# A hybrid decoder step on one core: the layer norms' rows written by ScalarE, row sums four at once, history products later

## The chip, the cores and the metric

The kernel runs on one core of a Trainium2 chip. The core has a matrix engine (TensorE: PE in the profile, with PEld for its weight loads), VectorE (DVE), ScalarE (ACT), GpSimd (POOL) and the queue engine SyncE (SP), which issues DMAs here. Each engine takes its own instructions in order, and semaphores hold one engine back for another. The metric is the device time of one execution in microseconds (us), as the median of several runs.

## The reference

The step computes two layers for 512 new prompt positions and 8 sampled sequences with one new token each, with a model width of 1024. Layer 0 mixes tokens by sliding-window attention, layer 1 by gated linear attention (GLA). Behind each mixer, and behind each gated convolutional feed-forward block (ConvFFN), stands a residual addition with a layer norm. There are four such norms, and they are what is changed:

```python
def layer_norm(x, g, b):
    mu = jnp.mean(xf, -1, keepdims=True)
    var = jnp.mean(jnp.square(xf - mu), -1, keepdims=True)
    return (xf - mu) * lax.rsqrt(var + LN_EPS) * g + b

def conv_ffn(x, buf, w_up, conv_w, conv_b, w_down):
    h = x @ w_up
    a, u = h[..., :D_FF], h[..., D_FF:]            # D_FF = 2816
    ap = jnp.concatenate([buf, a], axis=1)         # buf: the last 2 rows, the history
    c = conv_b + sum(conv_w[j] * ap[:, j:j + T] for j in range(3))
    return (gelu(c) * u) @ w_down, ap[:, T:]

for i in range(2):
    m = swa(x) if i == 0 else gla_mix(x)
    x = layer_norm(ALPHA * x + m, ln_mix_g[i], ln_mix_b[i])
    f, new_buf = conv_ffn(x, ...)
    x = layer_norm(ALPHA * x + f, ln_ffn_g[i], ln_ffn_b[i])
```

## The kernel before

**Layout.** The activations lie transposed: features on the 128 partitions, in 8 chunks of 128 features, and positions along the free dimension. Positions come in two groups: group a has 256 prompt positions, group b has 256 and the 8 sampled tokens (264 columns). For each group `g.x` holds the rows in f32; a high and a low part of each (`xh` and `xl`, for group a both in `xs`, in the type fp32r) feed TensorE. A weight is split in the same way (`wh`, `wl`), and a product is three matmuls for each chunk: high by high, high by low, low by high. The columns of the parts are stored in two halves by parity; `parted` and `even` are that view.

**Order.** The work is a list of units, one for each 128 columns of a weight; `order` runs each unit for group a some units ahead of group b (the lead). Generators (`spawn`, `yield n`) run a unit's later work n slots on. The instructions that come out are put in their engines' order by a planner that simulates the engines and lets each take what is ready; `issue_after` and `keep_in_program_order` bind it in single places. The time below is of the chip and not of that planner.

**A norm** is `ln_chunk` for each of the 8 chunks and then `ln_end`. `ln_chunk` adds the product to the residual (line 337 or 343), takes chunk 0's mean off all chunks (356), squares the chunk on ScalarE into `sq` (361), and adds the row and its square to two running sums `s1` and `s2` (373, 374; both print as `s_a` or `s_b` in the profile). Chunks below `p1` and `p2` are added on GpSimd and the others on VectorE: for group a `s1` is VectorE's and `s2` changes over at chunk 4, for group b (but in the last norm) both change over at chunk 7. `ln_end` sums over partitions by matmuls with a matrix of 1/1024 (381), forms the reciprocal root `rp` (397 to 414), and takes the mean off (403). It then writes each chunk in three steps: scale by `g` and `rp` on VectorE (441), add the bias and round to the high part on ScalarE (442), and bias plus row less high part on VectorE (443). `g.x` itself stays without its bias there. So the bias is added again where the rows are used later: through `self.back` in the next residual (line 337), by `shift` on GpSimd (457), and in the row sums.

**Row sums.** From the fifth FFN column block on, the two groups' products go through `ffn_pair`, a scheme with seven half products that needs sums and differences of the groups' rows. `row_sums` forms them chunk by chunk (475 to 501), with the difference of two biases in `step`; `row_sum1` splits the first of them.

**ConvFFN.** For the first four blocks `ffn_gate` copies TensorE's result to `aext` beside two columns of history, forms the three taps (804 to 810) and the GELU (815), and `ffn_value` multiplies (823, `hprod`) and splits. TensorE's results lie in four PSUM buffers (`accp`) that these readers free; four more hold `sc` (two buffers), `tp` and `pv` for everything small. `ffn_open` loads the sampled sequences' history `sconv` by a DMA on ScalarE's queue and forms its share of the convolution in `base` on GpSimd (776 to 780); the first reader is line 810.

**Weights.** SyncE loads them into two `raw` buffers. In the starts of the FFNs and of GLA, `parts` makes the high part on ScalarE (218), a negated copy of it on ScalarE (207), and adds the weight to that copy with a DMA on GpSimd's queue (208), which gives the low part.

Of the kernel before, what the change touches and what calls it, by code (L numbers as in the profile page):

```python
# [20 lines left out]
P = 128  # L21
# [37 lines left out]
LATEB = 14  # L59

HOLD = 6
# [39 lines left out]
class Net:  # L101
    def __init__(self, tc, ctx, I, O):
# [20 lines left out]
        self.back = c.tile([P, KD], F32, name="back")  # L123
# [204 lines left out]
    def ln_chunk(self, g, m, ps, scaled, last=False):  # L328
# [7 lines left out]
        if scaled:  # L336
            first = nc.vector.scalar_tensor_tensor(x[:, m], x[:, m], self.back[:, m:m + 1], ps, op0=ALU.add, op1=ALU.add)
            if m == 0 and g.i == 0:
                with self.tc.issue_after(first.ins):
                    for kind in self.kept:  # L340
                        self.release(kind)
        else:
            nc.vector.scalar_tensor_tensor(x[:, m], x[:, m], ALPHA, ps, op0=ALU.mult, op1=ALU.add)
# [16 lines left out]
        q = c("sq", 2)  # L360
# [10 lines left out]

        p1, p2 = (KD - 1, KD - 1) if g.i and not last else (0, S2P)
# [3 lines left out]
    def ln_end(self, g, i, last=False):  # L376
# [8 lines left out]
        mu, q, nv, r = t("mu"), t("msq"), t("nv"), t("r")  # L385
# [31 lines left out]
        if last:  # L417

            behind = None
            for m in range(0, KD, 2):  # L420
# [3 lines left out]
                for j in (m, m + 1):  # L424
                    if j in (0, 1, 2, 4, 6):
                        nc.scalar.activation(x[:, j], x[:, j], AF.Identity, scale=sc(j), bias=bi(j))
                    elif j == 3:
# [12 lines left out]
        for m in range(KD):  # L440
            v = nc.vector.scalar_tensor_tensor(x[:, m], x[:, m], sc(m), rp, op0=ALU.mult, op1=ALU.mult)
            nc.scalar.activation(g.xh[:, m], parted(x[:, m]), AF.Identity, bias=bi(m))
            xl = nc.vector.scalar_tensor_tensor(g.xl[:, m], parted(x[:, m]), bi(m), g.xh[:, m].bitcast(F32), op0=ALU.add, op1=ALU.subtract)
# [3 lines left out]
        if i % 2 == 0:  # L447
            if g.i:
                self.spawn(self.row_sums(i), 1)
            return  # L450
        for m in range(KD):
            yield 1 if m else LATEB
            self.shift(g, i, m)

    def shift(self, g, i, m):
        bi = self.par[:, C_LNB + i * KD + m:C_LNB + i * KD + m + 1]
        self.tc.keep_in_program_order(self.nc.gpsimd.tensor_scalar(g.x[:, m], g.x[:, m], 1.0, bi, op0=ALU.mult, op1=ALU.add))

    def row_sums(self, i):
# [6 lines left out]
        bias = lambda m: self.par[:, C_LNB + i * KD + m:C_LNB + i * KD + m + 1]  # L466
        step = self.pp.tile([P, half], F32, name="step")
        p0 = C_LNB + i * KD
        nc.gpsimd.tensor_tensor(step, self.par[:, p0 + half:p0 + KD], self.par[:, p0:p0 + half], op=ALU.subtract)
        wide = lambda t: t.rearrange("p (k c) -> p k c", k=half)  # L470
        even = lambda t: t.rearrange("p k (j t) -> p k t j", t=2)
        row = lambda g, k: g.x[:, k, 0:256]
        self.t1 = [self.ln.tile([P, NT - 256], F32, name=name, bufs=c)[:, :256] for name, c in (("sq", 2), ("sq", 2), ("mu", 1), ("msq", 1))]
        with self.tc.issue_after(self.rest):
            v.tensor_tensor(self.t1[0], row(a, 0), row(b, 0), op=ALU.subtract)
        for k in range(1, half):
            v.tensor_tensor(self.t1[k], row(a, k), row(b, k), op=ALU.subtract)
        yield 2
        with self.behind_chain():
            ts = self.pp.tile([P, 2, half, NS], F32, name="tsum")  # L480
            gap = step.unsqueeze(2).broadcast_to([P, half, NS])
            for q, x, y, op in ((0, lo, hi, ALU.subtract), (1, hi, lo, ALU.add)):
                v.tensor_tensor(ts[:, q], b.x[:, x, 256:], b.x[:, y, 256:], op=ALU.subtract)
                v.tensor_tensor(ts[:, q], ts[:, q], gap, op=op)
                self.split(self.th[q][:, :, :, n:], self.tl[q][:, :, :, n:], even(ts[:, q]))
            r = wide(self.pp.tile([P, KD * P], F32, name="raw", bufs=2))
            for k in range(half):
                v.scalar_tensor_tensor(r[:, k], row(b, half + k), bias(half + k), self.t1[k], op0=ALU.add, op1=ALU.add)
            th, tl = self.th[0][:, :, :, :n], self.tl[0][:, :, :, :n]
            nc.scalar.activation(th, even(r), AF.Copy, scale=-1.0)  # L490
            for k in range(half):
                v.scalar_tensor_tensor(tl[:, k], even(r)[:, k], -1.0, th[:, k].bitcast(F32), op0=ALU.mult, op1=ALU.subtract)
        yield 3
        with self.behind_chain():
            for k in range(half):
                v.scalar_tensor_tensor(r[:, k], r[:, k], bias(half + k), row(a, half + k), op0=ALU.subtract, op1=ALU.subtract)
            self.split(self.th[2], self.tl[2], even(r))
        yield 2
        with self.behind_chain():
            for k in range(half):  # L500
                v.scalar_tensor_tensor(r[:, k], row(b, half + k), step[:, k:k + 1], row(b, k), op0=ALU.add, op1=ALU.subtract)
            self.split(self.th[1][:, :, :, :n], self.tl[1][:, :, :, :n], even(r))

    def row_sum1(self):

        nc, b, n = self.nc, self.groups[1], P
        for k in range(KD // 2):
            self.split(b.xh[:, k, :, :n], b.xl[:, k, :, :n], parted(self.t1[k]))
        for r in (b.xh, b.xl):
            r = r[:, 0:KD // 2, :, n:]  # L510
# [244 lines left out]
    def ffn_open(self, layer):  # L755
# [4 lines left out]
        nc.scalar.dma_start(out=self.sconv, in_=self.I["state_conv"][layer])  # L760
# [5 lines left out]
        w = lambda j: self.par[:, C_CW + (layer * 3 + j) * NF:C_CW + (layer * 3 + j + 1) * NF].unsqueeze(2).broadcast_to([P, NF, NS])  # L766
        b = self.par[:, C_CB + layer * NF:C_CB + (layer + 1) * NF].unsqueeze(2).broadcast_to([P, NF, NS])
# [3 lines left out]
        self.cp, self.cp_cm = self.open(f"chain{layer}")  # L771
# [746 lines left out]
```

## Time and profile before

| | us |
|---|---|
| median of 3 runs | 1094.07 (1093.5 to 1095.92) |
| profiled execution | 1093.0 |
| its span, first to last instruction | 1091.1 |
| TensorE busy in it | 1058.5 (97%) |
| VectorE busy | 870.9 (80%) |
| ScalarE busy | 684.3 (63%) |
| GpSimd busy | 315.1 (29%) |
| TensorE clock granted | 0.995 |

A row of a timeline is start, duration, engine, line, operation, out<-in by the program's names, shape, count, and in brackets the engine's idle time before it with what ended it. Where several run back to back the duration is that of the whole row. A row of one line's instructions gives durations in ns as least, median and most. A row of waits gives total us, count and longest.

The mix norm of layer 0 lies at about 126 to 191 us, the FFN norm of layer 0 at 470 to 525, the mix norm of layer 1 at 699 to 763, and the last norm at 1043 to the end.

### The profile page before, as it was taken

To read this page: it belongs to the slowest core of one execution; us is meant where nothing else is said; L and a number is where in the kernel's file an instruction comes from. 1 tells how busy PE (TensorE), PEld (TensorE's weight loads), DVE (VectorE), ACT (ScalarE), POOL (GpSimd) and SP (SyncE) were. 2 spreads that over 40 slices of the span, in tenths; PEclk is the share of its full clock that TensorE was granted. 3 is DMA by queue.
4 is the path that set the end of the run, shared out by engine and by line. 5 is a ranking of instruction groups with operands and counts; after the bars stand their busy time and mean duration, and the time that the engine had idled before them with its cause. 6 is when DMAs were issued, how large, how long until landed. Compare 5 with 4: busy or idle time off the path is not lost. (4 is left out here: it accounts for less than half of the span.)

```text
span 1091.1 us, 23870 instructions
## 1 busy us (share of the span) xinstructions
PE 1058.5 (97%) x9174; PEld 1029.6 (94%) x9174; DVE 870.9 (80%) x1813; ACT 684.3 (63%) x1356; POOL 315.1 (29%) x512
## 2 busy tenths in 40 slices
PE   8999999999999999999999999989999999999996
PEld 7998899999999999999999999889999999999995
DVE  7898668988788778978766776687988788778975
ACT  5677657776655665647666756467776655665643
POOL 4476573221111110174221111362221111110163
PEclk9999999999999999999999999999999999999998
DMA  7454048588777775448235445368587777774322
GB/s 230 149 165 135 23 121 215 125 215 194 184 174 175 175 189 118 107 149 213 59 103 169 132 151 170 93 174 218 129 213 194 183 173 176 174 190 117 108 76 79
DMA packets 65474, 167.45 MB, mean 153 GB/s; under 512 B 8104, under 2 KB 28624, under 8 KB 65360
## 3 DMA queue, kind: packets, MB, share of 16 engines
q1 hardware_dynamic: 50960, 119.47, 34.2%
q0 software_dynamic: 12240, 44.57, 23.3%
q10 hardware_dynamic: 2160, 1.89, 0.5%
q8 instruction: 72, 1.18, 0.5%
q14 instruction: 42, 0.34, 0.1%
HBM read 153.24 MB, written 8.47 MB: 148 GB/s over the span
## 5 line engine op out<-in xcount | busy, mean ns | idle before, releaser
L315 ACT ACTIVATE wh<-raw 128x1024 fp32r<-128x1024 f32 x72 | 76.0, 1059 | 89.9 <-PE widep L929 44.7
L311 PE MATMUL widep<-tl,wh 128*128 128x264 f32 (+1 forms) x432 | 119.1, 276 | 0.0
L312 PE MATMUL widep<-th,wl 128*128 128x264 f32 (+1 forms) x432 | 119.1, 276 | 0.0
L310 PE MATMUL widep<-th,wh 128*128 128x264 f32 (+1 forms) x432 | 119.1, 276 | 0.0
L196 ACT ACTIVATE wh<-raw 128x1024 fp32r<-128x1024 f32 (+1 forms) x91 | 95.0, 1047 | 38.2 <-PE accp L240 11.8
L238 PE MATMUL accp<-xh_b,wh 128*128 128x264 f32 x400 | 113.2, 283 | 2.9 <-DVE hprod L823 2.4
L242 PE MATMUL accp<-xh_b,wl 128*128 128x264 f32 x400 | 111.8, 280 | 0.0
L208 POOL DMA_DIRECT2D wl<-in_w_down x28 | 24.3, 867 | 291.7 <-ACT wl L207 269.0
L240 PE MATMUL accp<-xl_b,wh 128*128 128x264 f32 x384 | 106.8, 278 | 0.0
L238 PE MATMUL accp<-xs_a,wh 128*128 128x256 f32 x400 | 104.9, 282 | 1.4 <-ACT wh L196 0.9
L240 PE MATMUL accp<-xs_a,wh 128*128 128x256 f32 x384 | 102.1, 282 | 0.5
L316 DVE TENSOR_TENSOR wl<-raw,wh 128x1024 fp32r<-128x1024 f32 x72 | 87.5, 1218 | 7.0 <-ACT wh L315 7.0
L207 ACT ACTIVATE wl<-wh 128x1024 fp32r<-128x1024 f32 x85 | 89.2, 1053 | 1.0
L202 DVE TENSOR_TENSOR wl<-raw,wh 128x1024 fp32r<-128x1024 f32 (+2 forms) x63 | 77.8, 1242 | 11.7 <-ACT wh L196 11.4
L310 PEld LDWEIGHTS widep<-th,wh 128*128 128x128 f32 x432 | 82.1, 190 | 0.0
L311 PEld LDWEIGHTS widep<-tl,wh 128*128 128x128 f32 x432 | 82.1, 190 | 0.0
L312 PEld LDWEIGHTS widep<-th,wl 128*128 128x128 f32 x432 | 82.1, 190 | 0.0
L238 PEld LDWEIGHTS accp<-xh_b,wh 128*128 128x128 f32 x400 | 75.7, 189 | 4.7 <-DVE hprod L823 3.2
L310 PE MATMUL widep<-xh_b,wh 128*128 128x264 f32 x288 | 79.6, 276 | 0.0
L311 PE MATMUL widep<-xl_b,wh 128*128 128x264 f32 x288 | 79.5, 276 | 0.0
L312 PE MATMUL widep<-xh_b,wl 128*128 128x264 f32 x288 | 79.5, 276 | 0.0
L238 PEld LDWEIGHTS accp<-xs_a,wh 128*128 128x128 f32 x400 | 76.3, 193 | 2.7 <-ACT wh L196 1.2
(424 smaller groups left out, 4000.7 us busy)
## 6 DMA issues: line engine op xcount, KB each, us to landing
raw<-in_w_up SPq DMA_DIRECT2D x88, 512.0 KB, 4.0
wl<-in_w_up POOLq DMA_DIRECT2D x52, 512.0 KB, 7.0
raw<-in_w_down SPq DMA_DIRECT2D x44, 512.0 KB, 3.7
wl<-in_w_down POOLq DMA_DIRECT2D x28, 512.0 KB, 6.6
raw<-in_w_gla SPq DMA_DIRECT2D x24, 512.0 KB, 3.5
raw<-in_w_mix_o SPq DMA_DIRECT2D x16, 512.0 KB, 4.2
qs<-hl SPq DMA_DIRECT2D x64, 64.0 KB, 2.1
sgla<-in_state_gla SPq DMA_DIRECT2D x16, 256.0 KB, 3.1
```

The lines of the kernel that those rows point to most:

```text
L196: nc.scalar.activation(h[:, c], r[:, c], AF.Copy)
L202: nc.vector.tensor_tensor(l[:, c], r[:, c], h[:, c].bitcast(F32), op=ALU.subtract)
L207: self.nc.scalar.activation(l, h.bitcast(F32), AF.Copy, scale=-1.0)
L208: self.nc.gpsimd.dma_start(out=l, in_=src, accum_op=ALU.add)
L238: nc.tensor.matmul(o, h[:, ks], xh, start=k == 0, stop=False)
L240: nc.tensor.matmul(o, h[:, ks], xl, start=False, stop=False)
L242: nc.tensor.matmul(o, l[:, ks], xh, start=False, stop=not tail and k == nt - 1)
L310: self.nc.tensor.matmul(o, h[:, ks], rh, start=k == 0, stop=False)
L311: self.nc.tensor.matmul(o, h[:, ks], rl, start=False, stop=False)
L312: self.final = self.nc.tensor.matmul(o, l[:, ks], rh, start=False, stop=k == KD // 2 - 1).ins
L315: self.nc.scalar.activation(hi, src, AF.Copy)
L316: self.nc.vector.tensor_tensor(lo, src, hi.bitcast(F32), op=ALU.subtract)
```

## The change

Six things are done together.

1. **Rows.** `ln_end` now works on two chunks at once. VectorE multiplies both by `rp`; ScalarE applies scale and bias to each chunk in place, so that `g.x` is the finished norm; ScalarE copies both to the high part; VectorE subtracts for both low parts.
2. **No later biases.** `back`, `shift` and `step` go. The residual of the FFN norms becomes a plain addition.
3. **Row sums** of four chunks in one instruction each. What were the four small buffers (`sq` twice, `mu`, `msq`) is now one tile `quad` of four rows.
4. **Squares.** `sq` goes to a PSUM buffer of `sc` for the chunks whose square VectorE adds (not for the last chunk of the last norm), and stays in `quad` where GpSimd adds it.
5. **History.** The load of `sconv` and the `base` products move to `ffn_base`, spawned three slots later and bound behind the last copy to a high part (`self.high`).
6. **Tail.** In the last norm, group b's chunk 5 is scaled on GpSimd instead of VectorE.

```diff
+        self.quad = self.ln.tile([P, 4, NT - 256], F32, name="quad")
...
-            first = nc.vector.scalar_tensor_tensor(x[:, m], x[:, m], self.back[:, m:m + 1], ps, op0=ALU.add, op1=ALU.add)
+            first = nc.vector.tensor_tensor(x[:, m], x[:, m], ps, op=ALU.add)
...
-        q = c("sq", 2)
+        p1, p2 = (KD - 1, KD - 1) if g.i and not last else (0, S2P)
+        q = self.quad[:, m % 2, :n] if m < p2 or last and m == KD - 1 else self.mtile("sc")[:, :n]
         sq = nc.scalar.activation(q, x[:, m], AF.Square)
...
-        mu, q, nv, r = t("mu"), t("msq"), t("nv"), t("r")
+        mu, q, nv, r = self.quad[:, 2, :n], self.quad[:, 3, :n], t("nv"), t("r")
...
-                    elif j == 3:
+                    elif j == 3 or j == 5 and g.i:
                         nc.gpsimd.tensor_scalar(x[:, j], x[:, j], sc(j), bi(j), op0=ALU.mult, op1=ALU.add)
...
-        for m in range(KD):
-            v = nc.vector.scalar_tensor_tensor(x[:, m], x[:, m], sc(m), rp, op0=ALU.mult, op1=ALU.mult)
-            nc.scalar.activation(g.xh[:, m], parted(x[:, m]), AF.Identity, bias=bi(m))
-            xl = nc.vector.scalar_tensor_tensor(g.xl[:, m], parted(x[:, m]), bi(m), g.xh[:, m].bitcast(F32), op0=ALU.add, op1=ALU.subtract)
+        for m in range(0, KD, 2):
+            ms = slice(m, m + 2)
+            v = nc.vector.tensor_tensor(x[:, ms], x[:, ms], rp.unsqueeze(1).broadcast_to([P, 2, n]), op=ALU.mult)
+            for j in (m, m + 1):
+                nc.scalar.activation(x[:, j], x[:, j], AF.Identity, scale=sc(j), bias=bi(j))
+            y = x[:, ms].rearrange("p k (j t) -> p k t j", t=2)
+            self.high = nc.scalar.activation(g.xh[:, ms], y, AF.Copy).ins
+            xl = nc.vector.tensor_tensor(g.xl[:, ms], y, g.xh[:, ms].bitcast(F32), op=ALU.subtract)
...
-        for m in range(KD):
-            yield 1 if m else LATEB
-            self.shift(g, i, m)
...
-        for k in range(1, half):
-            v.tensor_tensor(self.t1[k], row(a, k), row(b, k), op=ALU.subtract)
+            v.tensor_tensor(self.t1, row(a, lo), row(b, lo), op=ALU.subtract)
...
-            for k in range(half):
-                v.scalar_tensor_tensor(r[:, k], row(b, half + k), bias(half + k), self.t1[k], op0=ALU.add, op1=ALU.add)
-            th, tl = self.th[0][:, :, :, :n], self.tl[0][:, :, :, :n]
-            nc.scalar.activation(th, even(r), AF.Copy, scale=-1.0)
-            for k in range(half):
-                v.scalar_tensor_tensor(tl[:, k], even(r)[:, k], -1.0, th[:, k].bitcast(F32), op0=ALU.mult, op1=ALU.subtract)
+            v.scalar_tensor_tensor(r, self.t1, -1.0, row(b, hi), op0=ALU.mult, op1=ALU.subtract)
+            self.split(self.th[0][:, :, :, :n], self.tl[0][:, :, :, :n], even(r))
...
-            for k in range(half):
-                v.scalar_tensor_tensor(r[:, k], r[:, k], bias(half + k), row(a, half + k), op0=ALU.subtract, op1=ALU.subtract)
+            v.scalar_tensor_tensor(r, r, -1.0, row(a, hi), op0=ALU.mult, op1=ALU.subtract)
...
-            for k in range(half):
-                v.scalar_tensor_tensor(r[:, k], row(b, half + k), step[:, k:k + 1], row(b, k), op0=ALU.add, op1=ALU.subtract)
+            v.tensor_tensor(r, row(b, hi), row(b, lo), op=ALU.subtract)
...
+        self.spawn(self.ffn_base(layer), BASE)
+
+    def ffn_base(self, layer):
+        nc = self.nc
+        with self.tc.issue_after(self.high):
+            nc.scalar.dma_start(out=self.sconv, in_=self.I["state_conv"][layer])
...
         g = nc.gpsimd
-        b0 = C_LNB + 2 * layer * KD
-        g.tensor_scalar(self.back, self.par[:, b0:b0 + KD], ALPHA, 0.0, op0=ALU.mult, op1=ALU.add)
         g.tensor_tensor(self.base, self.sconv[:, :, :, 0], w(0), op=ALU.mult)
         g.tensor_tensor(t, self.sconv[:, :, :, 1], w(1), op=ALU.mult)
         g.tensor_tensor(self.base, self.base, t, op=ALU.add)
         g.tensor_tensor(self.base, self.base, b, op=ALU.add)
```

More of the change, by code (lines that the diff above doesn't have):

```diff
@@ L465, in row_sums @@
         v = nc.vector
[L466 to L470, printed above, removed]
         even = lambda t: t.rearrange("p k (j t) -> p k t j", t=2)
-        row = lambda g, k: g.x[:, k, 0:256]
-        self.t1 = [self.ln.tile([P, NT - 256], F32, name=name, bufs=c)[:, :256] for name, c in (("sq", 2), ("sq", 2), ("mu", 1), ("msq", 1))]
+        row = lambda g, ks: g.x[:, ks, 0:256]
+        self.t1 = self.quad[:, :, :256]
         with self.tc.issue_after(self.rest):
-            v.tensor_tensor(self.t1[0], row(a, 0), row(b, 0), op=ALU.subtract)
-        for k in range(1, half):
-            v.tensor_tensor(self.t1[k], row(a, k), row(b, k), op=ALU.subtract)
+            v.tensor_tensor(self.t1, row(a, lo), row(b, lo), op=ALU.subtract)
         yield 2
@@ L499, in row_sums @@
         with self.behind_chain():
-            for k in range(half):
-                v.scalar_tensor_tensor(r[:, k], row(b, half + k), step[:, k:k + 1], row(b, k), op0=ALU.add, op1=ALU.subtract)
+            v.tensor_tensor(r, row(b, hi), row(b, lo), op=ALU.subtract)
             self.split(self.th[1][:, :, :, :n], self.tl[1][:, :, :, :n], even(r))
     def row_sum1(self):
-        nc, b, n = self.nc, self.groups[1], P
-        for k in range(KD // 2):
-            self.split(b.xh[:, k, :, :n], b.xl[:, k, :, :n], parted(self.t1[k]))
+        nc, b, n, half = self.nc, self.groups[1], P, KD // 2
+        self.split(b.xh[:, :half, :, :n], b.xl[:, :half, :, :n], self.t1.rearrange("p k (j t) -> p k t j", t=2))
         for r in (b.xh, b.xl):
-            r = r[:, 0:KD // 2, :, n:]
+            r = r[:, 0:half, :, n:]
             nc.gpsimd.tensor_scalar(r, r.bitcast(F32), -1.0, 0.0, op0=ALU.mult, op1=ALU.add)
@@ L759, in ffn_open @@
         self.sconv = p.tile([P, NF, NS, 2], F32, name="sconv")
-        nc.scalar.dma_start(out=self.sconv, in_=self.I["state_conv"][layer])
         self.plain, self.chain = True, {}
@@ L780, in ffn_open @@
         g.tensor_copy(self.nconv_s[:, :, :, 0], self.sconv[:, :, :, 1])
+        yield from ()
     def behind_chain(self):
@@ L1213, in gla_g @@
         sg = self.gp.tile([P, NT - 256], F32, name="sg", bufs=3)[:, :n]
[L1214 removed]
+        d, r = (self.quad[:, 3, :n], self.ln.tile([P, NT - 256], F32, name="nv")[:, :n])
         nc.scalar.copy(sg, ps)
```

27 lines of the change are left out of this document (9 added, 18 removed).

## The prediction

> **What bounds the kernel now.** I read the page's engine table first, then the waits of TensorE, then the timelines of the engines around the norms, then busy time by stage.
>
> ```profile
> PE 1058.5 (97%) x9174; PEld 1029.6 (94%) x9174; DVE 870.9 (80%) x1813; ACT 684.3 (63%) x1356; POOL 315.1 (29%) x512
> ...
> PE accp L238 <- DVE hprod L823: 2.4, 4, 1.1
> PE accp L245 <- DMA wl<-in_w_up: 2.1, 4, 0.8
> PE pv L381 <- DVE s_a L374: 1.9, 1, 1.9
> PE accp L242 <- DMA wl<-in_w_up: 0.6, 2, 0.4
> PE accp L238 <- DVE q_a L1063: 0.5, 1, 0.5
> ```
>
> TensorE (PE) is busy 97% of the span, and the change removes no matmul. So only three things can move the time: PE's waits near the norms, new waits there, and the tail after the last matmul. The columns of the wait rows are total us, times, longest. The waits that the change can reach are: one for the sum of squares (`s_a`, 1.9), four for a PSUM bank that the FFN product `hprod` holds (2.4), six for low parts of weights (`wl`, 2.7), and one at the start of GLA (0.5). Together 7.5 us of 1091. A change that edits hundreds of vector instructions can therefore win at most some 7 us and the tail.
>
> **Squares in PSUM.** The 1.9 us wait is in layer 1's mix norm. The stalled instruction, what VectorE ran before it, and what GpSimd (POOL) was doing:
>
> ```profile
> 723.56 0.52 DVE L373 TENSOR_TENSOR s_a<-s_a,x_a 128x256 f32<-128x256 f32 x1
> 725.17 3.24 DVE L374 TENSOR_TENSOR s_a<-s_a,sq 128x256 f32<-128x256 f32 x1 [1.09 <-ACT sq L361]
> ...
> 727.41 0.71 POOL L777 TENSOR_TENSOR hprod<-sconv,par 128x176 f32<-128x176 f32 x1
> ...
> L374 DVE TENSOR_TENSOR s_a<-s_a,sq x15: 409/848/3242, 137.8 to 1060.8; 128x256 f32<-128x256 f32 x15
> L343 DVE SCALAR_TENSOR_TENSOR x_a<-x_a,accp x16: 403/407/422, 114.3 to 723.1; 128x256 f32<-128x256 f32 x16
> ```
>
> An addition that takes 0.41 us at best took 3.24, and it ended just after POOL's run did (727.41 + 0.71 = 728.12). The same-sized operation with one input in PSUM (`accp`) stays between 0.403 and 0.422 over 16 calls. After the change, `sq` of chunks 4 to 7 of group a lies in PSUM, so I price that addition at 0.41. It then ends at 725.6 in place of 728.4, 2.8 earlier against a wait of 1.9, so the wait goes: **−1.9** (ends 0 and −1.9). The `base` products (L777) leave this place too. What could be late next is the first-sum addition L373, which keeps two SBUF inputs. ScalarE's square itself I leave at its 0.42 us: no row has ScalarE writing PSUM. The squares take turns in the two `sc` buffers with the mean and the scores. Square 5 must then wait until VectorE has read square 4. That delays the second sum by at most one addition, 0.4; I take 0 and put 0.4 in the range.
>
> [...]
>
> **The normalised rows.** Per norm and group, these are the rows of before and the nearest rows for after:
>
> ```profile
> 161.26 3.22 DVE L441 SCALAR_TENSOR_TENSOR x_a<-x_a,par,pv 128x256 f32<-128x256 f32 x8
> 189.19 1.72 DVE L443 SCALAR_TENSOR_TENSOR xl_b<-x_b,par,xh_b 128x264 fp32r<-128x264 f32 x4
> 184.49 2.90 ACT L442 ACTIVATE xh_b<-x_b,par 128x264 fp32r<-128x264 f32 x6
> ...
> 157.27 2.47 DVE L403 TENSOR_TENSOR x_a<-x_a,tp 128x512 f32<-128x512 f32 x4
> L261 DVE TENSOR_TENSOR sum<-raw x36: 678/683/698, 200.5 to 1016.5; 128x512 f32<-128x512 f32 x36
> 1084.00 2.10 ACT L426 ACTIVATE x_b<-x_b,par 128x264 f32<-128x264 f32 x4 [2.20 <-DVE x_b L423]
> L888 ACT ACTIVATE conv<-conv x36: 621/638/645, 233.7 to 1038.5; 128x520 f32<-128x520 f32 x36
> ```
>
> VectorE: eight scalings (3.22) become four two-chunk products with a PSUM operand, like L403 (2.47). Eight low parts (2 × 1.72 = 3.4) become four two-chunk subtractions, like L261 (4 × 0.68 less overlap, some 2.5). That is 1.6 us less. ScalarE: eight `xh` (2.90/6 × 8 = 3.9) become eight scale-and-bias (2 × 2.10 = 4.2) and four two-chunk copies (4 × 0.64 less overlap, 2.2), or 6.4: 2.5 us more. This is the price of the change. VectorE loses about 9.6 us over six norms and ScalarE gains 15.
>
> Where this shows depends on what each is short of:
>
> ```profile
> 160.00:165.00 5.00, 5.00 (x47) 5.00 (x46) 4.93 (x14) 4.53 (x8) 3.31 (x5) 1.00 0.90 243
> 165.00:170.00 5.00, 5.00 (x47) 5.00 (x46) 5.00 (x10) 5.00 (x11) 2.74 (x4) 1.00 1.03 230
> 170.00:175.00 5.00, 5.00 (x43) 4.87 (x42) 1.72 (x4) 3.66 (x7) 2.71 (x4) 1.00 1.06 283
> 175.00:180.00 5.00, 5.00 (x47) 5.00 (x47) 5.00 (x11) 4.68 (x8) 1.39 (x4) 1.00 1.01 243
> 185.00:190.00 5.00, 4.61 (x41) 4.42 (x41) 5.00 (x15) 2.39 (x6) 0.00 (x0) 1.00 0.50 111
> 190.00:195.00 5.00, 4.46 (x40) 4.26 (x39) 4.87 (x17) 2.19 (x7) 0.83 (x4) 1.00 0.00 0
> ```
>
> (Columns: PE, PEld, DVE, ACT, POOL busy, clock, DMA share, GB/s.) In 160 to 180, group a's rows are written between ScalarE's splits of the first FFN weights. ScalarE has 2.1 us free of 20 there and the DMA engines none. An `xh` later by x delays a weight's split, its low-part DMA, and PE's `wl` wait. But the DMA engines are full already, so a split that comes 1 us later need not land 1 us later, and part of the extra 2.5 fits into the 2.1 free. I take +0.5 per FFN layer, **+1.0** in all; ends −1.0 (POOL, freed of the base products, issues the first low part earlier) and +5.0 (all of it, both layers).
>
> In 185 to 195, group b's rows, it is the reverse: VectorE is full and ScalarE half idle. There sit the `hprod` waits: VectorE does the two halves of a convolution with low parts and row sums between them.
>
> ```profile
> 765.30 0.42 ACT L815 ACTIVATE conv<-conv 128x256 f32<-128x256 f32 x1 [5.38 <-DVE conv L806]
> ```
>
> The row sums shrink as well:
>
> ```profile
> 191.18 0.41 DVE L477 TENSOR_TENSOR sq<-x_a,x_b 128x256 f32<-128x256 f32 x1
> 192.91 0.86 DVE L488 SCALAR_TENSOR_TENSOR raw<-x_b,par,sq 128x256 f32<-128x256 f32 x2
> 196.50 1.46 DVE L492 SCALAR_TENSOR_TENSOR tl<-raw,th 128x256 fp32r<-128x256 f32 x4 [0.93 <-ACT th L490]
> 198.99 1.28 DVE L496 SCALAR_TENSOR_TENSOR raw<-raw,par,x_a 128x256 f32<-128x256 f32 x3
> 202.25 1.23 DVE L316 TENSOR_TENSOR tl<-raw,th 128x1024 fp32r<-128x1024 f32 x1
> 204.13 1.68 DVE L501 SCALAR_TENSOR_TENSOR raw<-x_b,step 128x256 f32<-128x256 f32 x4
> ```
>
> Before: 1.6 (L477 and L475, four) + 1.7 (L488) + 1.5 + 1.7 (L496) + 1.7 = 8.2. After: five instructions of 128x1024 at 1.23 = 6.2. With the two small `step` additions gone, 2.3 less per layer. Before the late `hprod` stand the low parts, the first sums and the L488: 0.85 + 0.4 + 0.4 = 1.7 us less in front of it, against single waits of at most 1.1. ScalarE now paces `xl_b` (four pairs of 1.6 = 6.4, against VectorE's 6.6 for scalings and low parts before), which VectorE can fill with the convolution. I keep 0.7 of the 2.4: **−1.7** (ends −2.4 and +1.0).
>
> GLA's start has the same form, but there ScalarE carries the decay that PE's `q_a` wait hangs on: **+0.3** (ends −0.5, the whole wait, and +2.5, the whole extra).
>
> **No later bias additions; residual without a scalar.**
>
> ```profile
> L457 POOL TENSOR_SCALAR x_a<-x_a,par x8: 480/486/740, 528.1 to 563.9; 128x256 f32<-128x256 f32 x8
> 530.00:580.00 50.00, 49.77 (x413) 46.84 (x412) 34.85 (x100) 32.20 (x82) 12.00 (x17) 1.00 0.30 90
> ```
>
> Sixteen POOL instructions of 0.49 go (7.8 us), in a stretch where PE is busy 49.77 of 50: nothing. `back` and `step` on POOL: nothing, POOL is off the path. The 32 residual additions without a pointer scalar get no dearer than L343's 0.41, and all but the last stand behind matmuls: nothing.
>
> **Late history.** The five POOL instructions for `base` and their DMA move behind the last `xh_b`.
>
> ```profile
> sconv<-in_state_conv ACTq DMA_DIRECT2D x2, 176.0 KB, 2.5
> 194.24 0.21 DVE L810 SCALAR_TENSOR_TENSOR conv<-aext,par,base 128x8 f32<-128x8 f32 x1
> ```
>
> They leave a place where they kept POOL from group b's mean subtraction, but PE did not wait there: nothing. In the new place the last `xh_b` ends at 184.49 + 2.90 + 2.5 = 189.9. The landing (2.5) and five POOL instructions at L777's 0.71 make `base` ready at 195.9, where its first reader stood at 194.24. If the reader simply stands later in VectorE's order, it costs nothing; if VectorE waits in front of it, 1.7 per layer, and what queues behind L810 there, the next convolution and its `hprod`, comes late, for whose bank PE waits. On ScalarE's queue the DMA issue comes behind the `xh_b` that it waits for anyway; on POOL the history copies queue behind the products. I take **0**, because the order is planned with the load in it; ends 0 and +3.4.
>
> **Tail.**
>
> ```profile
> 1085.23 0.42 DVE L430 TENSOR_SCALAR x_b<-x_b,par 128x264 f32<-128x264 f32 x1
> 1085.56 0.70 DVE L423 TENSOR_TENSOR x_b<-x_b,pv 128x528 f32<-128x528 f32 x1
> 1086.30 0.61 ACT L426 ACTIVATE x_b<-x_b,par 128x264 f32<-128x264 f32 x1 [0.19 <-DVE x_b L423]
> ```
>
> Chunk 5 goes to POOL, so L423 moves up by 0.33 and ends at 1085.93. ScalarE is busy to 1086.10 (L426, above), so the last scale-and-bias and its output move up by 0.2: **−0.2** (ends −0.3 and 0).
>
> **The sum.** −1.9 + 1.0 − 1.7 + 0.3 + 0 − 0.2 = −2.5. The profiled execution took 1093.0 (span 1091.1 and 1.9 around it), the median of the runs is 1094.07, 1.07 above it. So the forecast is 1090.5 for such an execution and **1091.6** for the median.
>
> **Rivals.**
> - *More waits go* (0.15): all 4.3 of `s_a` and `hprod`, 1.3 of the 2.7 `wl`, the 0.5 of GLA and the tail, 6.3 in all: 1087.8. For it: VectorE is full at each. Against: ScalarE's 2.5 per norm.
> - *The wait only changes place* (0.15), no change. [...]
> - *ScalarE becomes the bound* (0.13), slower. In the FFN starts all 2.5 of group a's extra reaches the `wl` landings in both layers (+5.0) and no `hprod` wait goes: −1.9 + 5.0 + 0.3 − 0.2 = +3.2, 1097.3. It decides from 2.0 per layer on. For it: 5.00 of 5.00 in 165 to 170. Against: 1.34 idle in 170 to 175, and full DMA engines.
> - *`base` comes late* (0.07), slower: VectorE stands at L810 for 1.7 per layer, the `hprod` waits of 2.4 stay and grow by 3.4: −1.9 + 1.0 + 3.4 + 0.3 − 0.2 = +2.6, 1096.7. It decides from 1.5 per layer on. For it: VectorE takes its queue in order. Against: ScalarE's GELU, not PE, reads that part first.
>
> **How the numbers follow.** The forecast has 0.50, with its own range 1090 to 1093. From 0.2% (2.2 us, about what a measurement tells from no change) follow: faster 0.37 of the forecast's 0.50 and all of the first rival, 0.52; same 0.13 and the second rival, 0.28; slower the last two, 0.20. The range leaves out half of the first rival and most of the last two: 1087.5 to 1096.0.
>
> **What would show it.** The wait of `pv` for `s_a` gone, and L374 of group a at 0.41 for chunks 4 to 7; `hprod` waits under 1 us; L426-like scale-and-bias at 0.5 and copies at 0.64 on ScalarE, its sum up by some 15 and VectorE's down by 14; `wl` waits between 2.7 and 4.5; L810 without a wait for POOL. I am wrong if `wl` waits pass 6, if PE waits for `xs_a` or `xh_b`, or if another wait of 2 us stands where `s_a` stood.

## The result, and the profile after

The changed kernel takes **1110.55 us** (median of four runs, 1110.28 to 1112.25) against 1094.56 us for the kernel before beside it: a ratio of 1.015, 95% interval [1.0135, 1.0165]. It is 16 us slower, where 1091.6 was forecast. Between the two profiled executions the span grew by 17.7 us, from 1091.1 to 1108.8.

First the page of the kernel after, its engine table:

```profile
PE 1064.6 (96%) x9174; PEld 1034.9 (93%) x9174; DVE 851.6 (77%) x1724; ACT 701.0 (63%) x1374; POOL 312.6 (28%) x493
```

VectorE lost 19.3 us of work and ScalarE gained 16.7, close to the 14 and 15 that were forecast. TensorE has the same 9174 matmuls, and two things grew: its idle time (span less busy) from 32.6 to 44.2 us, and its busy time from 1058.5 to 1064.6 us. So 11.6 us are idle time, and 6.1 us are the same matmuls taking longer. The two need two explanations.

The waits of TensorE in the kernel after (total us, times, longest):

```profile
PE accp L242 <- DMA wl<-in_w_up: 3.8, 2, 2.1
PE tp L380 <- DVE s_b L372: 3.6, 3, 1.2
PE accp L238 <- ACT xs_a L445: 3.6, 2, 1.9
PE tp L1209 <- ACT on L1121: 3.4, 1, 3.4
PE accp L1003 <- issue: 2.9, 1, 2.9
...
PE accp L245 <- DMA wl<-in_w_up: 1.2, 1, 1.2
...
PE accp L238 <- DVE hprod L806: 0.4, 1, 0.4
PE tp L380 <- DVE s_a L372: 0.3, 1, 0.3
```

The last two rows are the waits that the change was to shorten, and they are shorter: `hprod` from 2.4 to 0.4, `s_a` from 1.9 to 0.3. The five rows at the top are new or larger. `xs_a` in rows three and five is group a's normalised high part, the input of the first product behind a norm. (The row `<- issue` is the same wait: its matmul reads `xs_a` and starts when the copy ends.) ScalarE's timeline at layer 0's first norm:

```profile
163.19 3.05 ACT L443 ACTIVATE x_a<-x_a,par 128x256 f32<-128x256 f32 x6
166.15 1.05 ACT L207 ACTIVATE wl<-wh 128x1024 fp32r<-128x1024 f32 x1
167.09 1.08 ACT L443 ACTIVATE x_a<-x_a,par 128x256 f32<-128x256 f32 x2
168.08 1.05 ACT L218 ACTIVATE wh<-raw 128x1024 fp32r<-128x1024 f32 x1
169.02 0.42 ACT L362 ACTIVATE quad<-x_b 128x264 f32<-128x264 f32 x1
169.34 0.65 ACT L445 ACTIVATE xs_a<-x_a 128x512 fp32r<-128x512 f32 x1
...
171.85 0.83 ACT L445 ACTIVATE xs_a<-x_a 128x512 fp32r<-128x512 f32 x1
```

and the two rows of TensorE's timeline there that have waits:

```profile
167.68 0.68 PE L380 MATMUL tp<-s_b,ones_a 128*128 128x264 f32 x2 [1.22 <-DVE s_b L372]
170.04 0.38 PE L238 MATMUL accp<-xs_a,wh 128*128 128x256 f32 x1 [1.68 <-ACT xs_a L445]
```

In ScalarE's planned order all eight scale-and-bias instructions (L443) and three pieces of other work stand ahead of the first copy (L445). The first high part is out at 169.99, 6.8 us after the rows began, and the last at 172.68, 9.5 us after. ScalarE's timeline in the kernel before, at the same place:

```profile
163.76 1.80 ACT L442 ACTIVATE xs_a<-x_a,par 128x256 fp32r<-128x256 f32 x4
...
168.31 1.05 ACT L442 ACTIVATE xs_a<-x_a,par 128x256 fp32r<-128x256 f32 x2
```

There ScalarE's first instruction was itself a high part, out after some 0.5 us; the last came 5.6 us after the start. At the other two norms the last high part of group a comes 9.2 and 11.1 us after the start, where it was 5.6 and 5.7. TensorE has matmuls of the phase before for the difference in the kernel before, and not for 4 us more. (`s_b`, group b's sum, comes into the list because the plan now puts group b's statistics ahead of group a's late product.)

For the 6.1 us of longer matmuls, busy time by stretches of 3.41 us (PE, PEld, DVE, ACT, POOL, granted clock, DMA share, GB/s) of the kernel after:

```profile
509.36:512.77 3.41, 0.82 (x6) 0.66 (x6) 0.83 (x1) 3.41 (x8) 2.08 (x3) 1.00 1.00 262
512.77:516.18 3.41, 3.41 (x16) 3.41 (x17) 2.52 (x4) 2.70 (x6) 0.92 (x2) 0.50 0.95 258
693.68:697.09 3.41, 0.30 (x1) 0.14 (x1) 1.44 (x6) 1.24 (x5) 0.00 (x0) 1.00 0.36 106
697.09:700.50 3.41, 3.37 (x14) 2.65 (x14) 2.51 (x6) 2.28 (x8) 0.00 (x0) 0.50 0.47 138
720.98:724.39 3.41, 1.98 (x13) 1.41 (x11) 2.91 (x9) 0.79 (x2) 0.00 (x0) 1.00 0.65 175
724.39:727.80 3.41, 3.33 (x13) 2.72 (x12) 2.07 (x5) 2.69 (x4) 0.00 (x0) 0.50 0.36 132
751.70:755.11 3.41, 1.51 (x9) 1.09 (x10) 0.74 (x1) 3.41 (x8) 1.34 (x2) 1.00 1.05 273
755.11:758.52 3.41, 3.41 (x18) 3.41 (x17) 1.84 (x3) 3.41 (x7) 0.45 (x2) 0.50 1.03 270
785.84:789.25 3.41, 1.27 (x11) 1.27 (x12) 3.41 (x8) 2.33 (x3) 1.45 (x2) 1.00 0.06 12
789.25:792.66 3.41, 3.41 (x19) 3.41 (x18) 1.37 (x4) 2.61 (x5) 1.84 (x3) 0.50 0.23 19
```

Five times a stretch in which TensorE was idle for much of the time is followed by 3.41 us at half clock, in which it gets through 13 to 19 matmuls where some 30 fit otherwise (30 in 205.58 to 208.99, at a clock of 1.00). The profile of the kernel before has none between its first 12 us and its tail. At a clock of 0.50 for 3.41 us, each such stretch loses up to 1.7 us by my estimate (half of 3.41): five make up to 8.5. That is more than the 6.1 of longer matmuls. One part of the difference is a stretch at half clock at 8.11 us that the kernel before has and the kernel after has not; the rest is not accounted for. It is not hidden by waits, for TensorE is busy during 3.33 to 3.41 us of each of the five.

Where the time was lost, from the start of each norm's first mean (L347), after minus before: layer 0's mix norm and its FFN +3.0 us (−0.8 to +2.2), layer 0's FFN norm and GLA +10.1 (to +12.3), layer 1's mix norm and its FFN +4.9 (to +17.2), the tail +0.5.

### The profile page after: what moved, and what is told of

It is laid out like the page before. It is cut to its first block, busy times and chain, and to the rows that moved or that the text cites. A ratio compares the mean times of both kernels' runs of the same rounds, so it can differ in the third digit from the quotient of the medians.

```text
span 1108.8 us, 23772 instructions
## 1 busy us (share of the span) xinstructions
PE 1064.6 (96%) x9174; PEld 1034.9 (93%) x9174; DVE 851.6 (77%) x1724; ACT 701.0 (63%) x1374; POOL 312.6 (28%) x493
## 3 DMA queue, kind: packets, MB, share of 16 engines
q10 hardware_dynamic: 2160, 1.89, 0.5%
## 4 chain that ended last, share of the span: by engine, by line
PE 75%; DVE 7%; ACT 7%; DMA 6%; issue 2%; POOL 1%; SPq 0%; DVEq 0%; ACTq 0%; POOLq 0%
PE widep L311 9%; PE widep L310 9%; PE widep L312 9%; PE accp L238 8%; PE accp L240 8%; PE accp L242 6%; PE widep L911 5%; PE widep L909 5%; PE widep L912 5%; PE accp L929 2%; PE onep L311 1%; PE onep L312 1%; PE onep L310 1%; PE accp L245 1%; DMA wl<-in_w_up 1%
## 5 line engine op out<-in xcount | busy, mean ns | idle before, releaser
L202 DVE TENSOR_TENSOR wl<-raw,wh 128x1024 fp32r<-128x1024 f32 (+2 forms) x63 | 78.1, 1248 | 17.8 <-ACT wh L196 16.7
L833 DVE TENSOR_TENSOR merged<-widep,conv 128x528 f32<-128x528 f32 x72 | 37.4, 562 | 57.2 <-PE widep L312 57.2
```

The lines of the kernel that those rows point to most:

```text
L202: nc.vector.tensor_tensor(l[:, c], r[:, c], h[:, c].bitcast(F32), op=ALU.subtract)
```

## The experiments

The theory (L): the loss lies in the new rows, because the path from the statistics to group a's high parts grew, and that gives the waits at the norms, an order planned later at the end of GLA, and the clock. Rivals: the squares in PSUM (S), the late history (H), the amount of ScalarE's work (W), the row sums or the missing bias additions (K).

**Squares and history undone, one by one and together.** Three kernels; in the first the squares:

```diff
-        q = self.quad[:, m % 2, :n] if m < p2 or last and m == KD - 1 else self.mtile("sc")[:, :n]
+        q = self.quad[:, m % 2, :n]
```

> The changed kernel with all squares in SBUF again (L361: q always a quarter of quad). Theory A: the squares are not what costs; one s_a wait of up to 1.9 us may come back, VectorE has up to 2.3 us more, so 1110 to 1114. Rival S, the two PSUM banks sc that the squares take hold up the work around them: the time falls by 5 us or more, to 1105 or below.

in the second the history's DMA and its five POOL operations back in `ffn_open`:

```diff
+        nc.scalar.dma_start(out=self.sconv, in_=self.I["state_conv"][layer])
...
-        self.spawn(self.ffn_base(layer), BASE)
```

> The changed kernel with the history of the convolution at the opening of the FFN again: its DMA and its five POOL operations are issued where they were before. Theory A: 1108 to 1112, the late history cost nothing that PE saw. Rival H, the late base (POOL to 195.3, ScalarE waits 2.24 us for L759, VectorE 0.76) costs 3 us or more a layer: the time falls to 1105 or below.

and in the third both:

> The changed kernel with both undone, squares in SBUF and the early history: what is left of the change is the rows by ScalarE, the low parts two chunks at once, the row sums four at once and no later bias additions. Theory A: the loss is in these, 1109 to 1114, and the waits for xs_a stand in all three norms. Rivals S and H together: 1094 to 1100.

Measured 1112.8 (ratio 1.0176 [1.015, 1.0202]), 1109.5 (1.015 [1.0123, 1.0177]) and 1110.14 (1.0154 [1.0123, 1.0185]). S and H fall: with both undone the whole loss is still there, in what is left of the change: the rows, the row sums and the missing bias additions.

**The squares alone, in the kernel before.**

```diff
-        q = c("sq", 2)
+        q = c("sq", 2) if m < p2 or last and m == KD - 1 else self.mtile("sc")[:, :n]
```

> The kernel before with one part of the change: squares of chunks that VectorE adds up go to PSUM. The prediction's first term: the wait for s_a of 1.9 us at 725 goes, and VectorE has about 2 us less to do per layer: 1.5 to 2.5 us faster than before, 0.998. Rival: the wait only changes its place, within 0.5 us of before.

Measured 1094.54 against 1093.72, 1.0003 [0.9992, 1.0015]: no gain, as the rival had it. The wait changed its place. Two rows of VectorE's timeline at 726:

```profile
727.93 1.89 DVE L372 TENSOR_TENSOR s_a<-s_a,x_a 128x256 f32<-128x256 f32 x1
729.74 0.41 DVE L373 TENSOR_TENSOR s_a<-s_a,sc 128x256 f32<-128x256 f32 x1
```

The addition that reads PSUM (`sc`) now takes 0.41, and the one that still reads twice from SBUF took 1.89 beside POOL's sums (1.00 us from 727.83, 0.99 from 728.53); TensorE waits 2.4 us for it. In the changed kernel the slow addition of that norm stands at L372 as well:

```profile
736.48 2.53 DVE L372 TENSOR_TENSOR s_a<-s_a,x_a 128x256 f32<-128x256 f32 x1
```

There TensorE waits only 0.3 us for it.

**The order of the rows alone.** The next pair's L443 only behind the copy of the pair before:

```diff
+            with self.tc.issue_after(self.high) if m else ExitStack():
                 for j in (m, m + 1):
                     nc.scalar.activation(x[:, j], x[:, j], AF.Identity, scale=sc(j), bias=bi(j))
```

> The changed kernel with one order added: ScalarE may scale and bias the next pair of chunks (L443) only behind the copy (L445) of the pair before. Nothing is computed otherwise. Theory A, the order of the rows: in the changed kernel six L443 (3.05 us) stand ahead of the first copy of group a and two more behind it, so the first xs_a comes at about 169.99 instead of 164.3, PE waits 1.7, 2.9 and 1.9 us for xs_a in three norms, and the clock rows of 0.5 that follow those waits cost about 1.7 us each. With the order the first copy should start about 2 to 3 us earlier, the three waits should fall below 3 us in sum, at least two of the five new rows of 0.5 should go, and the time should be 1099 to 1104. Rival W, ScalarE's longer work (16.7 us more) whatever its order: the time stays at 1109 to 1112. Rival G, the wait of 3.4 us at the end of the GLA (about 5 us with the clock) is apart from the rows: by it that wait stays where it is.

Measured 1111.96 (1.0165 [1.0136, 1.0194]): no gain. My first form of the theory, that the order alone is at fault, fell; the time is the one that W named. ScalarE's timeline shows why:

```profile
165.72 1.08 ACT L443 ACTIVATE x_a<-x_a,par 128x256 f32<-128x256 f32 x2
...
168.91 0.64 ACT L445 ACTIVATE xs_a<-x_a 128x512 fp32r<-128x512 f32 x1
...
178.21 0.74 ACT L445 ACTIVATE xs_a<-x_a 128x512 fp32r<-128x512 f32 x1
```

The first copy ends 3.8 us after the rows began in place of 6.8, but the last 13.2 us after in place of 9.5, as weight splits and group b's squares slip between the pairs. The single waits for `xs_a` shrank to at most 1.1 us and became more. The path has eight scalings and four copies, whatever their order. The wait at the end of GLA stayed at 3.6 us.

**The change divided by layers.** The FFN layers' input norms and row sums alone (GLA's rows and late biases, squares and history as before); and, in the kernel before, the rows of GLA's input norm alone, without the later bias additions on GpSimd that they make needless:

```diff
-        for m in range(0, KD, 2):
+        for m in range(KD if i % 2 else 0):     # GLA's input norm: rows as in the kernel before
+            ...
+        for m in range(0, 0 if i % 2 else KD, 2):
```

> The change in the FFN layers' input norms alone (even norms: new rows of both groups, row sums four at once). The GLA layer's input norms have the old rows and POOL's late bias additions, squares are in SBUF, the history is early. The loss of the rows-only kernel (about 16 us) is to be divided between this kernel and the next. Theory L: here the waits for xs_a (about 1.7 and 1.9 us), the two for wl (about 2 us) and two or three rows of clock at 0.5 (1.7 us each) stand; GLA's start and end are as before: 1099 to 1103. Rival K2, the row sums help or do nothing and the FFN's norms are covered: 1094 to 1097.

> The kernel before with one part of the change: the rows of the GLA layer's input norm by ScalarE into x, with the bias, in both groups, and no later bias additions. Theory L: the waits at the start of the GLA (about 1.2 and 2.9 us) and at its end (about 3.4 us), each with a row of clock at 0.5 behind it: 8 to 10 us slower than before, 1101 to 1104. Rival, the GLA's part only shows together with the FFN's late transfers: within 3 us of before.

Measured 1100.65 (1.0081 [1.0064, 1.0098]) and 1104.72 (1.0117 [1.0094, 1.0141]) against 1092.6 beside them: 8 and 12 us, each within or just above what L expected, and together more than the whole. The waits of TensorE that lead the list in the FFN kernel:

```profile
PE accp L238 <- ACT xs_a L450: 4.0, 2, 2.2
PE tp L380 <- DVE s_b L372: 2.4, 2, 1.2
```

and in the GLA kernel (`L1029 <- issue` is its wait for `xs_a`):

```profile
PE tp L1235 <- ACT on L1147: 3.6, 1, 3.6
PE accp L1029 <- issue: 2.3, 1, 2.3
```

The wait of 3.6 us at GLA's end appears with GLA's new rows and their missing bias additions, in a kernel with nothing else of the change, and not in the FFN kernel. In the FFN kernel the row sums are new too; what they cost or gain by themselves was not tried.

**Old rows in GLA, everywhere, or for group a alone,** with POOL adding the bias to x at once:

```diff
+        for m in range(KD if <i % 2 | True | g.i == 0> else 0):
+            v = nc.vector.scalar_tensor_tensor(x[:, m], x[:, m], sc(m), rp, op0=ALU.mult, op1=ALU.mult)
+            self.high = nc.scalar.activation(g.xh[:, m], parted(x[:, m]), AF.Identity, bias=bi(m)).ins
+            xl = nc.vector.scalar_tensor_tensor(g.xl[:, m], parted(x[:, m]), bi(m), g.xh[:, m].bitcast(F32), ...)
+            nc.gpsimd.tensor_scalar(x[:, m], x[:, m], 1.0, bi(m), op0=ALU.mult, op1=ALU.add)
```

> The changed kernel with the rows of the first norm of the GLA layer's input (odd norm, both groups) made as in the kernel before: VectorE scales and multiplies each chunk, ScalarE adds the bias into the high part, VectorE makes the low part; POOL then adds the bias to x (times 1, plus bias). The other norms keep the new rows. Theory L, the rows take longer from the statistics to the last high part (ScalarE 8 x 0.59 + 4 x 0.65 = 7.3 us in place of 8 x 0.53 = 4.2 us), PE stands at each norm, and the order that was planned behind the GLA's late rows puts three weight loads ahead of the fourth vb load: the start of the GLA (waits of 1.15 and 2.9 us) and its end (3.4 us) should come back to those of before, with three or four of the five rows at 0.5 (1.7 us each) gone: 1098 to 1102. Rival K, the missing POOL bias additions or the row sums moved the GLA's end: the wait of 3.4 us stays and the time is 1104 or more.

> The changed kernel with the rows of all norms but the last made as in the kernel before (POOL adds the bias to x right away). Row sums four at once, squares in PSUM and the late history stay. Theory L: the whole loss lies in the rows, 1090 to 1095. Rival K: the row sums four at once or the missing additions cost part of it, 1097 or more.

> The changed kernel with the rows of group a alone made as in the kernel before (POOL adds the bias to x right away); group b keeps the new rows. Theory L: PE stands for group a's rows, which no work covers, and not for group b's: all waits of PE for xs_a L445 go, the two waits of about 2 us for wl in the FFNs shrink to about 1, but the planned order at the end of the GLA is as in the changed kernel (three weight loads ahead of the fourth vb), so its 3.4 us and its clock row stay: 1097 to 1102. Rival W, ScalarE's amount of work: half of the extra work is left, half of the loss stays, 1102 to 1105, and waits for xh_b appear.

Measured 1105.58 (1.0114 [1.009, 1.0139]), 1102.17 (1.0074 [1.005, 1.0097]) and 1107.11 (1.0115 [1.0089, 1.0141]). All three are faster than the changed kernel, the first and the third only just (their intervals touch its 1.0135), and all three miss L's numbers by 4 to 7 us. By their times the first two lie where K had put them, the first without the wait of 3.4 us that K asks for. The waits of 2.9 and 3.4 us at GLA's start and end went with GLA's old rows in both groups; those for ScalarE's `xs_a` went where group a had old rows. Part of what remains is of the experiment's own making, POOL's additions right behind the rows. VectorE's timeline in the kernel with old rows everywhere:

```profile
508.41 3.96 DVE L443 SCALAR_TENSOR_TENSOR xs_a<-x_a,par,xs_a 128x256 fp32r<-128x256 f32 x4
```

and in the kernel before, at the same norm:

```profile
505.19 2.57 DVE L443 SCALAR_TENSOR_TENSOR xs_a<-x_a,par,xs_a 128x256 fp32r<-128x256 f32 x4
```

The same four low parts take 1.4 us more beside POOL's additions (four of those, 2.59 us, from 510.54), and a wait of 2.6 us for a low part of a GLA weight ends at 530.64. That all of the 8 to 9 us left in the kernel with old rows comes from this was not tried, so the row sums are not cleared. In the kernel with group a's old rows, PE waits 2.8 and 3.8 us for `xh_b` instead, the sign that W had named: group b's rows need cover too.

**The bias to x behind the high parts, on ScalarE.** Old rows, no POOL additions; ScalarE adds the biases in place behind the last high part:

```diff
+            self.high = nc.scalar.activation(g.xh[:, m], parted(x[:, m]), AF.Identity, bias=bi(m)).ins
+        with self.tc.issue_after(self.high):
+            for m in range(KD):
+                nc.scalar.activation(x[:, m], x[:, m], AF.Identity, bias=bi(m))
```

> The changed kernel with the rows made as in the kernel before (VectorE scales, ScalarE adds the bias into the high part, VectorE the low part), and ScalarE adding the bias to x in place only behind the last high part. ScalarE does 8 x 0.53 + 8 x 0.59 = 9.0 us per norm and group, more than the changed kernel's 7.3, but the last high part is out after 4.2 us. Theory L, the path from statistics to high part is what costs: the waits for xs_a go and the time falls to 1096 to 1102 (the planned order at the GLA's end, with its 3.4 us wait, stays). Rival W, the amount of ScalarE's work: 1109 or more.

Measured 1104.95 (1.0117 [1.0102, 1.0132]), between the two theories. Its waits:

```profile
PE accp L245 <- DMA wl<-in_w_up: 6.2, 3, 2.7
PE tp L1216 <- ACT on L1128: 3.7, 1, 3.7
PE accp L242 <- DMA wl<-in_w_up: 3.2, 1, 3.2
```

With the high parts ahead, the waits for group a's rows at the norms are gone, though ScalarE does more work than in the changed kernel: L's half. But the waits for the weights' low parts, whose splits queue behind on ScalarE, are 9.4 us, where they were 2.7 in the kernel before: W's half. ScalarE near a norm had no room for the 3 us more ahead of the high parts, nor for nearly 5 more behind them.

The middle row is the wait at GLA's end. It stands here with old rows and early high parts, so their lateness is not what it needs. Over all runs there is none where POOL adds the bias to the rows of GLA's input norm in both groups (the kernel before, the FFN kernel, old rows in GLA and everywhere), and it is there, at 2.6 to 3.7 us, where ScalarE adds it in at least one. Whether ScalarE's extra work or POOL's missing additions bring it about was not separated.

**The end of GLA.** In the changed kernel VectorE's timeline, with what ended the idle time before each row:

```profile
687.51 1.23 DVE L202 TENSOR_TENSOR wl<-raw,wh 128x1024 fp32r<-128x1024 f32 x1 [2.42 <-ACT wh L196]
...
688.99 0.87 DVE L1182 SCALAR_TENSOR_TENSOR sgla<-vb,kraw,sgla 128x256 f32<-128x256 f32 x2
...
694.21 0.88 DVE L1182 SCALAR_TENSOR_TENSOR sgla<-vb,kraw,sgla 128x256 f32<-128x256 f32 x2 [1.92 <-DMA vb<-dv]
695.00 0.16 DVE L1128 TENSOR_SCALAR gsmall<-gsmall 128x2 f32<-128x2 f32 x1
```

TensorE's transposes wait for `on`, ScalarE's `on` for the small L1128, and that stands in VectorE's queue behind a state update that waits for a `vb` transfer. I took SP's queue for the cause, where three weight loads had come to stand ahead of that transfer, and held the last two back:

```diff
-            nc.sync.dma_start(out=r[:, c], in_=src[:, c])
+            pin = self.tc.keep_in_program_order if <w_mix_o of layer 1, 6 or 7> else lambda x: x
+            pin(nc.sync.dma_start(out=r[:, c], in_=src[:, c]))
```

> The changed kernel with one order added on SP's queue: the loads of the last two of the GLA layer's output weights (w_mix_o 6 and 7) stay behind the transfers that are issued ahead of them in the program, so the fourth vb of the third head has no such load that waits for a free raw buffer ahead of it beyond the sixth. Theory Q, the wait of 3.44 us at 693 comes from that queue: the wait falls below 1.5 us and the row of clock at 0.5 at 697 goes, the rest stays: 1104 to 1108. Rival, ScalarE or VectorE are late there for themselves: the wait stays, 1109 or more.

Measured 1125.48 (1.0306 [1.029, 1.0321]). Only 0.8 us of the wait went, and the two held loads came too late for their products (waits of 4.0 and 3.3 us for `wh`). The queue was not the main cause. The chain of the changed kernel ahead of the row at 694.21 (start, us, step) shows what came before:

```profile
689.38 0.48 DVE sgla L1182
...
689.89 4.29 DMA vb<-dv
```

The transfer takes 4.29 us and started right behind the update that frees its buffer (689.38 to 689.86); SP had issued the weight loads ahead of it by 689.1. VectorE had been given that update behind a weight split that waited 2.42 us for ScalarE (the row at 687.51). In the kernel before, that update ran at 674.59, ahead of the split. So VectorE's planned order is another one here, some 180 us behind GLA's rows. Why the plan comes out so is open.

**The clock.** Matmuls without use in two of the waits that a half-clock stretch followed:

```diff
+            mm = nc.tensor.matmul(e, self.ones_a, sums, start=True, stop=rest is None)
+            if e is e1 and g.i and not last:
+                with self.tc.issue_after(mm.ins):
+                    for _ in range(5):
+                        nc.tensor.matmul(tp[:, 384:512], self.ones_a, self.ident, start=True, stop=True)
```

> The changed kernel with five matmuls without use (128 columns, fp32, into free columns of the statistics' bank) between group b's first statistics and group a's first product in three norms, where PE waits 1.7, 2.9 and 1.9 us for xs_a. They take about 1.2 us of PE and lengthen nothing as long as they fit into the wait. Theory C, the clock falls to 0.5 for 3.41 us behind each stretch of 3.41 us in which PE was busy less than about half the time (0.24 and 0.44 ahead of the rows at 512.8 and 755.1): those two rows go, the other three stay, 3.4 us less: 1105 to 1108. Rival, the rows at 0.5 lie where PE would have waited anyway: 1110 to 1112, or more if the fillers delay the product.

Measured 1107.31 (1106.58 to 1108.27; 1.0127 [1.0114, 1.014]), 3.2 us below the changed kernel's 1110.55, with work added. The same stretches in it:

```profile
510.50:513.91 3.41, 1.60 (x15) 1.44 (x14) 0.49 (x1) 3.41 (x8) 1.69 (x3) 1.00 0.97 237
513.91:517.32 3.41, 3.38 (x31) 3.19 (x30) 3.07 (x5) 3.34 (x6) 0.98 (x2) 1.00 1.06 261
...
752.84:756.25 3.41, 2.67 (x23) 2.44 (x22) 1.08 (x2) 3.41 (x7) 1.64 (x2) 1.00 0.94 237
756.25:759.66 3.41, 3.41 (x33) 3.41 (x33) 1.62 (x3) 3.41 (x6) 0.89 (x2) 1.00 0.94 243
```

31 and 33 matmuls at full clock where the changed kernel had 16 and 18. The product behind the wait at GLA's start comes as late as before (3.6 us after the statistics in both), so what is won there lies behind the wait, in the clock. This profile has two stretches fewer in all: those at 512.77 and 755.11 are gone, and that at 789 too, one at 135.0 came, and the ones at GLA's end and at 725 stay. The 3.2 us agree with 1.7 for each of two stretches, but they are not the clock's alone, for the waits for `wl` fell from 5.0 to 2.8 as well.

The same in the kernel before, at its longest wait:

> The kernel before with six such matmuls ahead of group a's statistics in the second FFN's input norm, where PE waits 1.94 us for s_a and was busy 0.476 of the stretch without a row of 0.5 behind it. Theory C: in some executions that stretch falls below the edge and costs 1.7 us; with the matmuls it never does: 0.3 to 1.7 us faster in the median, and no row of 0.5 near 728. Rival: the matmuls (about 1.4 us) end behind the wait's end and cost up to 1 us; or the stretch never falls below: within 0.5 us of before.

Measured 1092.49 against 1093.6, 0.9992 [0.9976, 1.0007]: not to be told from no change. No version here beats the kernel before.

## Why the prediction was wrong

- **The normalised rows: the step that failed.** The prediction priced ScalarE's extra work as +1.0, through the weights' low parts alone, and took the high parts as they came: "ScalarE now paces `xl_b`" for group b, nothing for group a. The instruction costs were right (16.7 us more on ScalarE, 19.3 less on VectorE). What was missing is the time from statistics to the first and the last high part. It can be had from the prediction's own rows: 2 × 2.10 + 2.2 = 6.4 us on ScalarE where 3.9 stood, with each pair's copy behind its scalings, in the window 160 to 180 where it has 2.1 us free of 20. By that alone each norm's last high part is 2.5 us later, and more by what stands between; counted from ScalarE's first row instruction it came 3.6 to 5.4 us later in the three norms. The rows of the FFN norms (with the row sums) cost 8 us alone and those of GLA's norm (with the missing bias additions) 12, where the sum had +1.0 and +0.3. How much of that is the later high parts, and how much ScalarE's longer work, stays open: with the high parts early and ScalarE's work kept, some 12 of the 16 us were left. The text named a wait for `xs_a` as what would prove it wrong, and gave it no price.
- **The order was taken for pair by pair.** The planned order has all eight scalings first. By that the first high part came 6.8 us after the rows began, but the pairwise kernel shows that the loss does not hang on it.
- **wl waits: +1.0 forecast, from 2.7 to 5.0 measured in the rows shown, +2.3;** within the ends of −1.0 and +5.0.
- **GLA start: +0.3, ends −0.5 and +2.5.** Measured 2.9 for `xs_a` and 1.15 for `s_b` ahead of it, against the 0.5 of before: +3.5, above the upper end, which counted ScalarE's extra instructions only.
- **GLA's end had no term at all:** 3.4 us of wait, from an order planned anew. With GLA's rows and missing bias additions alone it is there; which of the two brings it is open.
- **The clock had no term:** five stretches, up to 8.5 us by their length, with 6.1 us of longer matmuls measured in all. The forecast could not have had its size from the trace of before, which has waits of up to 1.94 us and no such stretch in its middle; it could have had it as a risk, for in that trace's tail a stretch with 0.48 us of 3.41 busy (from 1079.89) is followed by a clock of 0.50.
- **hprod: −1.7 forecast, −2.0 measured.** Right in size; which of the shorter instructions did it was not tried. In the kernel with old rows everywhere, which has the same row sums, a wait of 1.7 us for `hprod` stands.
- **s_a: −1.9 forecast, −1.6 measured, but not by the mechanism given.** The squares in PSUM move the slow addition to L372 (1.89 us in the kernel with the squares alone, 2.53 in the changed one), the first sum, which the prediction named as what could be late next, and alone they gain nothing (1.0003), so the forecast's size came out partly by luck. In the changed kernel the wait is gone with either the squares or the late history left in, and 1.8 us again with both undone (single profiles).
- **Late history 0:** right, to within the 1 us that these runs tell. The **tail**'s term is right as far as it goes: the last scale-and-bias ends 3.34 us after the last norm's first product with `rp`, where it was 3.65. From the last norm's first mean to the end it is still 0.5 longer, as the span ends 5.1 us after that instruction and not 4.2; why is open.
- **The rival "ScalarE becomes the bound"** was nearest in kind. At 1097.3 it counted the `wl` landings only, and of those the measured 5.0 us of waits are 2.3 more than before, not 5.0 more.

## What to carry to other kernels

Price a moved operation twice: by what it adds to its engine's busy time, and by what it adds between the last statistic and the first matmul that needs the result. The second was some 4 to 5 us per norm here; the first came back as 9.4 us of waits for low parts when the work was moved behind the high parts. On a TensorE that is busy 97% of the span, a new wait of 2 us can cost 3.7 by my estimate from the changed kernel's five stretches, the wait and up to 1.7 behind it (3.41 us at a clock of 0.50). So find out which waits leave little busy time in a stretch of 3.41 us: here the four with 0.30 to 1.51 us were all followed by half clock. And where the instruction order is planned as a whole, an edit can cost at a place that it does not touch, so look at one-part kernels before explaining any of it.

## What the runs showed of the hardware

The five half-clock stretches of the changed kernel begin at 512.77, 697.09, 724.39, 755.11 and 789.25 us: 54, 8, 9 and 10 times 3.413 us apart. So in this profile they all lie on one grid of 3.413 us. Ahead of them TensorE was busy for 0.82, 0.30, 1.98, 1.51 and 1.27 us of 3.41. In two of these pieces the longest wait is only 1.90 (ending at 754.23) and 2.15 us (ending at 787.98). The following were not followed by half clock, of the changed kernel

```profile
202.17:205.58 3.41, 1.74 (x17) 1.54 (x15) 3.22 (x7) 3.41 (x5) 2.43 (x4) 1.00 0.88 145
205.58:208.99 3.41, 3.41 (x30) 3.41 (x31) 3.15 (x5) 1.73 (x3) 0.16 (x1) 1.00 0.81 143
```

and of the kernel before

```profile
724.87:728.28 3.41, 1.66 (x13) 1.41 (x12) 3.11 (x1) 0.27 (x1) 3.25 (x8) 1.00 0.56 88
728.28:731.69 3.41, 3.22 (x26) 3.17 (x27) 2.59 (x6) 2.32 (x5) 2.72 (x5) 1.00 0.34 66
```

In these two profiles, from 20 us to the tail, nine pieces of the grid at full clock have less than 2.0 us busy. The four with 0.30 to 1.51 us were followed by half clock, and of the five with 1.66 to 1.98 us one was, the one with 1.98 us and 13 matmuls (720.98). Nor does the busy time of a profile alone tell what follows. In the kernel before, 2.50 us busy from 4.69 was followed by a clock of 0.50 from 8.11, and in the kernel with the idle-filling matmuls this piece by half clock at 135.0:

```profile
131.62:135.03 3.41, 2.40 (x22) 2.25 (x20) 3.02 (x8) 1.44 (x5) 3.41 (x6) 1.00 0.02 5
```

Some 1.86 of its 2.40 us are, as an estimate, sixteen matmuls of only 16 columns each, which take 1.86 us both in the kernel before (from 132.47) and in the changed kernel (from 131.68). The grid lies differently in the profiles (an edge at 512.77 in the changed kernel's, at 513.91 in that of the kernel just named). A wait of 1.15 us for `hl_b` stands in a piece with 1.98 us busy that is followed by half clock in the changed kernel's profile; in the kernel before's the same wait of 1.16 us, in a piece with 2.25 us busy (from 707.84), is not followed by one. Whether the grid or the smaller waits beside it make that difference was not tried.
